# A decoder layer with sparse attention: one list schedule for the whole kernel, buffers that stay, and Strassen's algorithm in the second product of the MLP

## The chip, the cores and the metric

The kernel runs on one core of one Trainium2 chip. The metric is the time of one execution on the device in microseconds (us); the lower, the better. TensorE multiplies matrices into eight banks of PSUM, VectorE, ScalarE and GpSimd work on elements, and SyncE issues most DMAs.

## The reference

One decoder layer on 1024 tokens of width 1024, in float32. A conditioning vector gives shift, scale and gate for two sub-layers.

```
h    = rms_norm(x) * (1 + scale1) + shift1
proj = h @ w_in                              # queries, three kinds of keys and values, gates, convolution
attn = nsa_attention(...)                    # 8 heads: compressed, selected and windowed keys
conv = bgate * conv3(cgate * u)
x    = x + gate1 * (concat(attn, conv) @ w_out)
h2   = rms_norm(x) * (1 + scale2) + shift2
ff   = square(relu(h2 @ w_ff1)) @ w_ff2      # 1024 -> 4096 -> 1024
out  = x + gate2 * ff
```

## The kernel before

**Layout.** Everything is transposed: a tile has 128 channels on the partitions and tokens along the free dimension. The 1024 tokens are two halves of 512, called half 0 and half 1. A product in fp32 is made of three fast ones: each operand is split into a high part (a cast to fp32r, `P.copy`) and a low part (the operand less the high part, `P.sub`, on VectorE), and `mm3` issues high x high, high x low and low x high into one bank. So a tile of 128 x 512 with an inner dimension of 1024 is 8 x 3 = 24 matmuls of 128x128 by 128x512, and each tile of weights that comes by DMA costs a cast (ScalarE) and a subtraction (VectorE).

**Order of the work.** The code does not issue instructions itself. The calls `P.mm`, `P.act`, `P.tt`, `P.dma` and so on put operations into the plan (`class Plan`), with a cost for each engine on which they may run; the plan keeps which operation must follow which, from the regions of memory that they read and write, so that reusing a buffer makes an order too. `P.issue()` orders all the operations that have come since the last call: it runs a list schedule forward and one backward in turn, eight times, takes the time that was left to the end in one pass as the priority of the next, keeps the order with the shortest modelled span, and issues the instructions in it. Each engine then works through its own queue in order.

**Stages.** The plan is issued twice. The first plan holds the projections, the compressed keys and values, the convolution (`conv_fills`), the attention (`supers`: all of half 0, then half 1) and, as a filler that has no order of its own against the attention of half 1, `first_half`: for half 0 the output projection, the second norm, and tiles 2 to 31 of the hidden layer (`NFF = 30`), whose 128x512 results go to DRAM (`d_hid`). It ends with the output projection of half 1 (`out_proj`) and a copy of the eight tiles `x1h` (half 0 after the first sub-layer) into `FA1`. Then the pool `first` with the buffer `FA2` and the banks `sc`, `fa`, `po`, `stb` is closed, and new ones are opened: hidden tiles `hid` and the banks `pd`.

The second plan is the MLP. It finishes the second norm of half 1, and then goes through the hidden layer in four chunks of 8 tiles: `ff1` makes the tiles of half 1 (and tiles 0 and 1 of half 0; the others of half 0 come back from DRAM), each is split, and then eight output tiles are made for both halves with 24 matmuls each, and added with the gate `mod` into `x1` (`P.stt`, line 358 in the helper). In the first chunk `ada_cols` makes the last eight columns of the gates. After the fourth chunk the outputs are stored.

**Lines.** Nearly all operations are recorded in helpers: line 312 is a matmul, 315 a transposition, 336 a cast or copy on ScalarE, 338 on VectorE, 347 an addition, subtraction or product of two tensors on VectorE, 358 a product with a scalar and a sum on VectorE, 330 a function on ScalarE, 397 a DMA.

Of the kernel before, what the change touches and what calls it, by code (L numbers as in the profile page):

```python
# [10 lines left out]
F = mybir.dt.float32  # L11
R = mybir.dt.float32r
AF = mybir.ActivationFunctionType
ALU = mybir.AluOpType
PSUM = bass.MemoryType.PSUM
# [15 lines left out]
S_ = np.s_  # L31


def f32(ap):
    return ap.bitcast(F)
# [398 lines left out]
H0, H1, WR, RAN = 0, 8192, 16384, 16384 + 11328  # L434
AHEAD = {"silu": 30000}
FA1N, FA2N = 13316, 10752

NFF = 30


@with_exitstack
def hymba_layer(ctx: ExitStack, tc: tile.TileContext, xT, cT, w_first, w_cols, w_vg, w_ada, w_ada2, b_ada,
                norm1, norm2, qn, kn, pe, cw1, cw2, conv_w, rel_bias, onehot, ident_c, pair_c, w_out,
                w_ff1, w_ff2, out, dbg=None):
    nc = tc.nc
    P = Plan(tc)
    P.ahead = AHEAD
    mult, add, subt, amax, amin = ALU.mult, ALU.add, ALU.subtract, ALU.max, ALU.min
    EW = ("DVE",)

    def pool(stack, name, side="left", space=None):
        kw = {"space": space} if space else {"side": side}
        if space != DRAM:
            kw["reuse_waits"] = "tile"
        return stack.enter_context(tc.tile_pool(name=name, bufs=1, **kw))
# [7 lines left out]
    def mm3(ps, w, h, wsl, hsl, start, stop):  # L463
        P.mm(ps, w[0][wsl], h[0][hsl], start, False)
        P.mm(ps, w[0][wsl], h[1][hsl], False, False)
        P.mm(ps, w[1][wsl], h[0][hsl], False, stop)
# [9 lines left out]
    d_conv = [[dtile(f"d_conv{j}{i}", 128, 512) for i in range(2)] for j in range(4)]  # L476
# [3 lines left out]
    d_hid = [dtile(f"d_hid{j}", 128, 512) for j in range(32)]  # L480
# [8 lines left out]
    bones = ctile("bones", 128, dtype=R)  # L489
    mod, bad = ctile("mod", 48), ctile("bad", 48)  # L490
    n1, n2, a1, a2, c1, ct, sl = (ctile(n, 8) for n in ("n1", "n2", "a1", "a2", "c1", "ct", "sl"))
    qnr, qns, knr, kns, eps, one = (ctile(n, 1) for n in ("qnr", "qns", "knr", "kns", "eps", "one"))
    cvw = ctile("cvw", 4, 3)
    gates = ctile("gates", 8, 24)
    vc = [ctile(f"vc{g}", 128, dtype=R) for g in range(2)]
# [3 lines left out]
    RA = keep.tile([128, RAN], R, name="RA")  # L499
    FA1 = keep.tile([128, FA1N], F, name="FA1")  # L500
    first = ctx.enter_context(ExitStack())
    FA2 = pool(first, "first", side="right").tile([128, FA2N], F, name="FA2")
    psp = pool(first, "ps", space=PSUM)
    sc_t = [psp.tile([128, 512], F, name=f"sc{i}") for i in range(4)]
    fa_t = [psp.tile([128, 512], F, name=f"fa{i}") for i in range(2)]
    po_t, stb = psp.tile([128, 512], F, name="po"), psp.tile([128, 512], F, name="stb")
# [5 lines left out]
    h = [[Region(RA, H0 + 8192 * hf + 4096 * i, H0 + 8192 * hf + 4096 * i + 4096)(8, 512) for i in range(2)] for hf in range(2)]  # L512
# [7 lines left out]
    def rsqrt_neg2(y, t, ms):  # L520

        P.act(t, ms, AF.Ln, bias=eps[0:t.shape[0]])
        P.act(y, t, AF.Exp, scale=-0.5)
        P.act(t, y, AF.Square)
        P.stt(t, ms, EPS, t, add, mult)
        P.stt(y, t, -3.0, y, add, mult)
        return y
# [34 lines left out]
    def ada_cols(j0, n, stage, acc, bank):  # L562

        for k in range(8):
            wa = stage()[:, 0:128 * n]
            P.dma(wa, w_ada2[k, :, 128 * (j0 - 16):128 * (j0 - 16 + n)])
            if k == 0:
                P.act(acc, wa, AF.Copy, scale=sl[:, k:k + 1])
            elif k % 2 == 0:
                P.stt(acc, wa, sl[:, k:k + 1], acc, mult, add)  # L570
            else:
                P.act(wa, wa, AF.Copy, scale=sl[:, k:k + 1])
                P.tt(acc, acc, wa, add, EW)
        for i in range(n):
            P.mm(bank[:, i:i + 1], acc[:, 128 * i:128 * i + 128], one, True, True)
        P.tt(mod[:, j0:j0 + n], bank[:, 0:n], bad[:, j0:j0 + n], add)
# [42 lines left out]
    for k in range(8):  # L619
# [5 lines left out]
        ws = wfs_r()  # L625
# [32 lines left out]
    banks, cbanks = Rot(sc_t), Rot([po_t, fa_t[0], fa_t[1]])  # L658
# [195 lines left out]
    while c0 < TROW:  # L854
        n = min(512, TROW - c0)
        a = cbanks()
# [24 lines left out]
    Gr = Region(FA2, 0, FA2N - 640)  # L881
    x1h, at0 = [Gr(512) for _ in range(8)], [Gr(512) for _ in range(4)]
    ot_r, ada_acc, ada_r = Gr.rot(2, 256), Gr(512), Gr.rot(3, 512)
    cg_t, z_t, t1_t = ([Dr(n) for _ in range(2)] for n in (512, 514, 512))

    Wr = Region(RA, WR, RAN)
    fw0_r, hl_r, kall0, q0_r, vt0 = Wr.rot(3, 2, 512), Wr.rot(8, 512), Wr(KC0 + T), Wr.rot(2, 2, 2, 256), Wr(4, 2, 128)
    Wr = Region(RA, RAN - 4160, RAN)
# [180 lines left out]
    def norm2_apply(k, t, x, y, h2):  # L1069
        P.tt(t, x, y, mult, EW)  # L1070
        P.act(t, t, AF.Identity, bias=mod[:, 24 + k:25 + k], scale=a2[:, k:k + 1])
        P.copy(h2[0][:, k], t, ("DVE", "ACT"))
        P.sub(h2[1][:, k], t, f32(h2[0][:, k]), EW)

    def first_half():
# [33 lines left out]

        tiles = [(w_ff1[j], lambda a, j=j: put_hid(j, a)) for j in range(32 - NFF, 32)]  # L1110
        P.group = "ff"
# [44 lines left out]
                    pass  # L1156


    x1 = [[FA1[:, 1024 * c + 512 * hf:1024 * c + 512 * hf + 512] for hf in range(2)] for c in range(8)]
    h2 = [h[0], h[1]]  # L1160
    tmp, sacc = Rot(at0), t1_t[1]
    wt_r = Region(RA, RAN - 4160, RAN).rot(4, 2, 512)
    for c in range(8):
        P.dma(x1[c][1], xT[c, :, 512:1024])
# [6 lines left out]
    for k in range(4):  # L1171
        load_mix(1, k, [ada_acc, *ada_r.t][k], h[1][0][:, k], h[1][1][:, k])
    out_proj(wt_r, h[1], Rot(sc_t), done_second)
    for c in range(8):
        P.dma(x1[c][0], x1h[c])
    P.issue()
    if dbg:
        for i in range(2):
            nc.sync.dma_start(out=dbg["vc"][i], in_=f32(vc[i]))
        nc.sync.dma_start(out=dbg["gates"], in_=gates)  # L1180
        for p in range(4):
            for m in range(2):
                nc.sync.dma_start(out=dbg["conv"][p * 128:p * 128 + 128, m * 512:m * 512 + 512], in_=d_conv[p][m])
        for c in range(8):
            for hf in range(2):
                nc.sync.dma_start(out=dbg["x1"][:, c, hf * 512:hf * 512 + 512], in_=x1[c][hf])
    first.close()


    with ExitStack() as pf:  # L1190
        ff = pool(pf, "ff", side="right")
        psd = pool(pf, "psD", space=PSUM)
        banks = Rot([psd.tile([128, 512], F, name=f"pd{i}") for i in range(8)])
        Fr, Gr = Region(FA1, 8192, FA1N - 1536), Region(FA1, FA1N - 1024, FA1N)
        ws_r = Fr.rot(2, 8, 128)
        tmp, ff_acc = Rot([*Fr.rot(3, 512).t, Gr(512)]), Gr(512)
        w5 = [Region(RA, c, c + 1024)(8, 128) for c in (*range(RAN - 4160, RAN - 1023, 1024), WR)]
        wh_r, wl_r = Rot([w5[0], w5[2], w5[4]]), Rot([w5[1], w5[3]])
        Wr = Region(RA, WR + 1024, RAN - 4160)
        hids = [Wr(512) for _ in range(12)] + [ff.tile([128, 512], R, name=f"hid{i}") for i in range(20)]  # L1200
        hid = [[[hids[16 * hf + 2 * j + i] for hf in range(2)] for j in range(8)] for i in range(2)]

        def load_w(src):
            ws, hi, lo = ws_r(), wh_r(), wl_r()
            P.dma(ws, src)
            P.copy(hi, ws)
            P.sub(lo, ws, f32(hi), EW)
            return hi, lo

        def split_hid(j, hf, t):  # L1210
            P.copy(hid[0][j][hf], t, ("DVE",))
            P.sub(hid[1][j][hf], t, f32(hid[0][j][hf]), EW)

        def ff1(j, hf, w):
            a = banks()
            for k in range(8):
                mm3(a, w, h2[hf], S_[:, k], S_[:, k], k == 0, k == 7)
            t = tmp()
            P.act(t, a, AF.Relu)
            P.act(t, t, AF.Square)  # L1220
            split_hid(j, hf, t)

        st, y1 = banks(), ff_acc
        P.mm(st, f32(bones), sacc, True, True)
        rsqrt_neg2(y1, tmp(), st)
        for k in range(8):
            norm2_apply(k, tmp(), x1[k][1], y1, h[1])
        for ch in range(4):
            for j in range(8):
                w = load_w(w_ff1[ch * 8 + j])  # L1230
                if ch * 8 + j >= 32 - NFF:
                    t = tmp()
                    P.dma(t, d_hid[ch * 8 + j])
                    split_hid(j, 0, t)
                else:
                    ff1(j, 0, w)
                ff1(j, 1, w)
            if ch == 0:
                for i in range(2):
                    ada_cols(40 + 4 * i, 4, tmp, ff_acc, banks())  # L1240
            for c in range(8):
                w = load_w(w_ff2[ch, c])
                for hf in range(2):
                    a = banks()
                    for k in range(8):
                        hh = [hid[i][k][hf] for i in range(2)]
                        mm3(a, w, hh, S_[:, k], S_[:], k == 0, k == 7)
                    P.stt(x1[c][hf], a, mod[:, 40 + c:41 + c], x1[c][hf], mult, add)
                    if ch == 3:
                        P.dma(out[c, :, hf * 512:hf * 512 + 512], x1[c][hf])  # L1250
        P.issue()

# [78 lines left out]
```

## Time and profile before

| | before |
|---|---|
| time, median of 3 runs | 1353.28 us (1350.94 to 1354.62) |
| profiled execution | 1352.0 us, span 1350.2 us |
| TensorE busy | 1322.4 us (98%), 6424 matmuls |
| VectorE busy | 776.7 us (58%) |
| ScalarE busy | 626.6 us (46%) |
| mean granted clock of TensorE | 0.994 |
| DMA | 175.63 MB, mean 130 GB/s |

The span goes from the first to the last instruction of the profiled execution; the time contains what lies around it, too. A busy time is the union of an engine's instructions. Matmuls overlap in the records: one of 128x512 lasts some 0.39 us there, and the next starts before it ends, so the distance between starts says how dense TensorE is. The same holds, less strongly, on VectorE.

### The profile page before, as it was taken

Reading aid. Unit: us, or ns where it says so; the run is one execution under the profiler, and the core shown is the slowest. Engines: PE = TensorE matmul, PEld = TensorE weight load, DVE = VectorE, ACT = ScalarE, POOL = GpSimd, SP = SyncE. Lnnn points to the kernel's source line nnn. Section 1 sums busy time; section 2 is a strip of 40 time slices with the busy share of each in tenths; the row PEclk is TensorE's granted clock in tenths of the full one; section 3 lists DMA queues with packets and bytes.
Section 4 is the critical chain, followed back from the end, with each engine's and each line's share of the span. In section 5 each row is a group of like instructions: output and inputs, shape, how many; then the busy total and the mean of one; then the engine's idle time right before and its main releaser. Section 6 shows DMA issues by size and latency. Waiting matters only on the chain.

```text
span 1350.2 us, 18276 instructions
## 1 busy us (share of the span) xinstructions
PE 1322.4 (98%) x6424; PEld 1079.6 (80%) x6424; DVE 776.7 (58%) x1882; ACT 626.6 (46%) x1294; POOL 131.5 (10%) x239
## 2 busy tenths in 40 slices
PE   6999999999999999999999999999999999999998
PEld 2788788878878878888888877888888888888887
DVE  6998778868587696565655447543522342244312
ACT  6776677666565597565665435320221032103200
POOL 0001003222221112121112000000000000000000
PEclk9999999999999989999999999999999999999999
DMA  9488895444251315334225523532322241223231
GB/s 331 156 238 237 278 312 186 146 154 135 89 172 57 112 33 169 108 119 145 94 86 172 159 60 102 166 107 86 116 80 61 66 123 63 63 78 94 76 111 63
DMA packets 91601, 175.63 MB, mean 130 GB/s; under 512 B 10746, under 2 KB 30755, under 8 KB 90997
## 3 DMA queue, kind: packets, MB, share of 16 engines
q1 hardware_dynamic: 87764, 159.65, 37.7%
q0 software_dynamic: 3744, 14.81, 3.5%
q8 instruction: 50, 0.82, 0.2%
q14 instruction: 43, 0.34, 0.1%
HBM read 145.48 MB, written 32.61 MB: 132 GB/s over the span
## 4 chain that ended last, share of the span: by engine, by line
PE 88%; DVE 6%; DMA 3%; issue 1%; ACT 1%; SPq 0%; POOL 0%; DVEq 0%; ACTq 0%; POOLq 0%
PE pd L312 39%; PE fa L312 23%; PE sc L312 15%; PE po L312 6%; PE stb L315 3%; PE sc L315 2%; DVE FA L358 2%; DVE RA L347 1%; DVE FA L347 1%; ACT FA L330 1%; DVE FA L377 1%; DMA FA<-in_w_ada 1%; DMA d_tab<-d_row 0%; SPq L397 0%; DMA d_k<-FA 0%
## 5 line engine op out<-in xcount | busy, mean ns | idle before, releaser
L312 PE MATMUL fa<-RA 128*128 128x512 f32 (+1 forms) x1384 | 448.0, 410 | 1.0 <-DVE RA L338 0.7
L312 PE MATMUL pd<-RA 128*128 128x512 f32 x1392 | 409.0, 390 | 0.6 <-DVE RA L338 0.5
L336 ACT CAST RA<-FA 128x512 fp32r<-128x512 f32 (+5 forms) x237 | 163.8, 707 | 459.0 <-PE pd L312 273.0
L312 PE MATMUL sc<-RA 128*128 128x512 f32 (+7 forms) x1328 | 352.3, 367 | 6.8 <-ACT RA L336 2.6
L347 DVE TENSOR_TENSOR RA<-FA,RA 128x512 fp32r<-128x512 f32 (+5 forms) x327 | 248.9, 777 | 141.0 <-PE pd L312 68.4
L312 PE MATMUL pd<-hid,RA 128*128 128x512 f32 x960 | 309.7, 389 | 0.0
L312 PEld LDWEIGHTS pd<-RA 128*128 128x128 f32 x1392 | 261.0, 188 | 56.1 <-issue 1.4
L312 PEld LDWEIGHTS fa<-RA 128*128 128x128 f32 (+1 forms) x1384 | 249.0, 190 | 43.9 <-DVE RA L338 0.9
L312 PEld LDWEIGHTS sc<-RA 128*128 128x128 f32 x1328 | 234.7, 190 | 50.3 <-DVE RA L347 4.6
L312 PEld LDWEIGHTS pd<-hid,RA 128*128 128x128 f32 x960 | 180.2, 188 | 37.4
L358 DVE SCALAR_TENSOR_TENSOR FA<-pd,mod,FA 128x512 f32<-128x512 f32 x64 | 46.4, 746 | 199.8 <-PE pd L312 199.8
L312 PE MATMUL po<-RA 128*128 128x256 f32 (+2 forms) x564 | 140.2, 302 | 0.0
L330 ACT ACTIVATE FA<-FA,nm 128x64 f32<-128x64 f32 (+6 forms) x192 | 114.9, 601 | 24.4 <-DVE nm L366 23.7
L312 PEld LDWEIGHTS po<-RA 128*128 128x128 f32 (+1 forms) x564 | 102.4, 190 | 13.4 <-issue 0.2
L377 DVE CUSTOM_DVE_ANT_0 FA<-sc,FA 128x64 f32<-128x64 f32 (+5 forms) x192 | 84.6, 455 | 43.9 <-PE sc L312 41.3
L330 ACT ACTIVATE FA<-FA 128x512 f32<-128x512 f32 (+2 forms) x147 | 89.9, 619 | 22.3 <-DVE FA L358 12.4
L370 POOL TENSOR_SCALAR FA<-FA,cf 128x640 f32<-128x640 f32 (+8 forms) x115 | 72.6, 642 | 238.5 <-DVE cf L347 136.2
L315 PE MATMUL stb<-FA,FA 128*128 128x128 f32 (+1 forms) x304 | 76.7, 279 | 3.0 <-DVE RA L347 3.0
L347 DVE TENSOR_TENSOR RA<-stb,RA 128x512 fp32r<-128x512 f32 (+1 forms) x84 | 53.3, 635 | 27.9 <-PE po L312 13.2
L315 PE MATMUL sc<-FA,FA 128*128 128x128 f32 (+1 forms) x288 | 68.0, 276 | 0.0
L347 DVE TENSOR_TENSOR RA<-sc,RA 128x512 fp32r<-128x512 f32 (+2 forms) x84 | 51.1, 608 | 25.5 <-ACT RA L336 14.4
L336 ACT CAST RA<-sc 128x512 fp32r<-128x512 f32 (+2 forms) x84 | 43.6, 519 | 38.3 <-PE sc L315 35.3
(126 smaller groups left out, 909.8 us busy)
## 6 DMA issues: line engine op xcount, KB each, us to landing
FA<-in_w_ff SPq DMA_DIRECT2D x64, 512.0 KB, 3.7
FA<-in_w_ada SPq DMA_DIRECT2D x64, 256.0 KB, 3.2
FA<-in_w_ff SPq DMA_DIRECT2D x60, 256.0 KB, 3.0
FA<-in_w_cols SPq DMA_DIRECT2D x34, 256.0 KB, 3.2
FA<-in_xT SPq DMA_DIRECT2D x32, 256.0 KB, 5.2
FA<-in_w_ada SPq DMA_DIRECT2D x16, 512.0 KB, 6.8
d_q<-FA SPq DMA_DIRECT2D x32, 256.0 KB, 4.2
RA<-d_q POOLq DMA_DIRECT2D x16, 512.0 KB, 5.3
```

The lines of the kernel that those rows point to most:

```text
L312: self.op([("PE", c, lambda: self.nc.tensor.matmul(out, a, b, start=start, stop=stop))], [out], [a, b])
L315: self.op([("PE", 110.0, lambda: self.nc.tensor.transpose(out, a, ident))], [out], [a, ident])
L330: self.op([("ACT", c, lambda: self.nc.scalar.activation(out, a, func, **kw))], outs, ins)
L336: alts.append((e, 0.833 * n + (53 if ps else 93), lambda: self.nc.scalar.copy(out, a)))
L347: alts.append((e, 1.04 * n + 68, lambda: self.nc.vector.tensor_tensor(out, a, b, op)))
L358: self.op([("DVE", 1.04 * self._n(out) + 68 + 61 * ptr, lambda: self.nc.vector.scalar_tensor_tensor(out, a, s, b, op0, op1, **kw))], [out] ...
L370: alts.append((e, 0.833 * n + 174 + 83 * ptr, lambda: self.nc.gpsimd.tensor_scalar(out, a, s1, s2, op0, op1)))
L377: self.op([("DVE", 1.04 * self._n(out) + 75, lambda: self.nc.vector.tensor_tensor_reduce(out, a, b, 1.0, init, ALU.add, ALU.max, accum))], ...
```

## The change

There is one plan and one `P.issue()` for the whole kernel. The pool `first` is not closed; the MLP takes its buffers from regions of `RA`, `FA1` and `FA2`, and its banks are the eight of the first stage in rotation. The tiles `x1h` stay where they are. `NFF` is 32: all tiles of half 0's hidden layer are part of `first_half`, and the MLP's loop reads all of them from DRAM. The weights of the first product are loaded in two parts of 128x512 (4 inner tiles each) instead of one of 128x1024.

The second product of a chunk is made by Strassen's algorithm (in the form with seven products and combinations that are used again). The chunk's weights are a 2 x 2 matrix of quarters (inner tiles 0 to 3 and 4 to 7, output tiles 0 to 3 and 4 to 7), the hidden tiles too (`b11`, `b21` are half 0, `b12`, `b22` half 1, inner tiles 0 to 3 and 4 to 7). In each of seven rounds four right-hand tiles are split (`split_b`), for each of four output tiles a quarter of weights is loaded and, in four rounds, added to or subtracted from another, split, and multiplied (`product`: 4 inner tiles, 12 matmuls). The bank is added with the gate into one or two output tiles, or into `u2`, which gathers the sum of the first and fourth rounds over all chunks and is added to three quarters of the output in the last chunk.

```diff
-NFF = 30
+NFF = 32
...
-    x1 = [[FA1[:, 1024 * c + 512 * hf:1024 * c + 512 * hf + 512] for hf in range(2)] for c in range(8)]
+    x1 = [[x1h[c], FA1[:, 512 * c:512 * c + 512]] for c in range(8)]
...
-    tmp, sacc = Rot(at0), t1_t[1]
+    tmp, sacc = Region(FA1, 4096, 6144).rot(4, 512), t1_t[1]
...
-    for c in range(8):
-        P.dma(x1[c][0], x1h[c])
-    P.issue()
-    first.close()
...
+    banks = Rot([*sc_t, *fa_t, po_t, stb])
+    raw = [at0 + Region(FA2, 6144, 8192).rot(4, 512).t, Region(FA1, 4096, 8192).rot(8, 512).t]
+    Fr = Region(FA2, 8192, FA2N)
+    u2, y1 = Fr.rot(4, 512).t, Fr(512)
+    Fr = Region(FA1, 8192, 12288)
+    st_r, S = Fr.rot(4, 512), Fr.rot(4, 512).t
+    st_r = Rot(st_r.t + Region(FA1, FA1N - 1024, FA1N).rot(2, 512).t)
+    Wr = Region(RA, WR, RAN)
+    w_r = Wr.rot(14, 512)
+    b_r = Rot([Wr(2, 4, 512), *Region(RA, H0, H0 + 8192).rot(2, 2, 4, 512).t])
+    def split(t):
+        hi, lo = w_r(), w_r()
+        P.copy(hi, t)
+        P.sub(lo, t, f32(hi), EW)
+        return [x.rearrange("p (k n) -> p k n", k=4) for x in (hi, lo)]
...
+    def split_b(tiles):
+        b = b_r()
+        for k, t in enumerate(tiles):
+            P.copy(b[:, 0, k], t, ("ACT", "DVE"))
+            P.sub(b[:, 1, k], t, f32(b[:, 0, k]), EW)
+        return b[:, 0], b[:, 1]
+    def product(w, x):
+        a = banks()
+        for k in range(4):
+            mm3(a, w, x, S_[:, k], S_[:, k], k == 0, k == 3)
+        return a
+    def ff1(j, hfs):
+        a = {hf: banks() for hf in hfs}
+        for kk in range(2):
+            w = split(load(st_r(), w_ff1[j][:, 4 * kk:4 * kk + 4]))
+            for hf in hfs:
+                for k in range(4):
+                    mm3(a[hf], w, h2[hf], S_[:, k], S_[:, 4 * kk + k], kk + k == 0, kk == 1 and k == 3)
+        for hf in hfs:
+            t = raw[hf][j % 8]
+            P.act(t, a[hf], AF.Relu)
+            P.act(t, t, AF.Square)
+    def to_out(c, hf, bank, sign=mod):
+        g = ng[:, c - 4:c - 3] if sign is ng else mod[:, 40 + c:41 + c]
+        P.stt(x1[c][hf], bank, g, x1[c][hf], mult, add)
...
+    for ch in range(4):
+        for j in range(8 * ch, 8 * ch + 8):
+            if j >= 32 - NFF:
+                P.dma(raw[0][j % 8], d_hid[j])
+                ff1(j, (1,))
...
+        if ch == 0:
+            for i in range(2):
+                ada_cols(40 + 4 * i, 4, st_r, y1, banks())
+            P.ts(ng, mod[:, 44:48], -1.0, None, mult)
+        b11, b12, b21, b22 = raw[0][0:4], raw[1][0:4], raw[0][4:8], raw[1][4:8]
+        def quad(c, f, k, t=None):
+            return load(st_r() if t is None else t, w_ff2[ch, c + 4 * f][:, 4 * k:4 * k + 4])
+        x = split_b(b11)
+        for c in range(4):
+            a = product(split(quad(c, 0, 0)), x)
+            if ch == 0:
+                P.copy(u2[c], a, ("DVE",))
+            else:
+                P.tt(u2[c], a, u2[c], add)
+            to_out(c, 0, a)
+        x = split_b(b21)
+        for c in range(4):
+            to_out(c, 0, product(split(quad(c, 0, 1)), x))
+            if ch == 3:
+                store(c, 0)
+        for k in range(4):
+            P.tt(b11[k], b12[k], b11[k], subt)
+        x = split_b(b11)
+        for c in range(4):
+            P.tt(S[c], quad(c, 1, 0, S[c]), quad(c, 1, 1), add)
+            a = product(split(S[c]), x)
+            to_out(c + 4, 1, a)
+            to_out(c, 1, a)
+        for k in range(4):
+            P.tt(b11[k], b22[k], b11[k], subt)
+        x = split_b(b11)
+        for c in range(4):
+            P.tt(S[c], S[c], quad(c, 0, 0), subt)
+            P.tt(u2[c], product(split(S[c]), x), u2[c], add)
+            if ch == 3:
+                to_out(c, 1, u2[c])
+                for hf in range(2):
+                    to_out(c + 4, hf, u2[c])
+        x = split_b(b22)
+        for c in range(4):
+            P.tt(S[c], quad(c, 0, 1), S[c], subt)
+            to_out(c, 1, product(split(S[c]), x))
...
+        for k in range(4):
+            P.tt(b12[k], b22[k], b12[k], subt)
+        x = split_b(b12)
+        for c in range(4):
+            t = quad(c, 0, 0)
+            P.tt(t, t, quad(c, 1, 0), subt)
+            a = product(split(t), x)
+            for hf in range(2):
+                to_out(c + 4, hf, a)
...
+        for k in range(4):
+            P.tt(b21[k], b11[k], b21[k], subt)
+        x = split_b(b21)
+        for c in range(4):
+            to_out(c + 4, 0, product(split(quad(c, 1, 1)), x), ng)
...
+    P.issue()
```

## Rows read from the trace of the kernel before

**Rows 1.** Stretches: span, busy TensorE, weight loads, VectorE, ScalarE, GpSimd, clock, DMA, GB/s.

```profile
33.80:67.50 33.70, 31.57 (x130) 23.62 (x129) 32.21 (x68) 25.18 (x45) 0.53 (x4) 0.97 0.50 156
67.50:101.20 33.70, 33.53 (x188) 28.58 (x187) 30.70 (x71) 23.96 (x52) 2.39 (x4) 1.00 0.84 238
...
202.00:472.00 270.00, 269.31 (x1464) 219.87 (x1463) 201.49 (x657) 166.93 (x436) 66.25 (x124) 1.00 0.41 132
472.00:510.00 38.00, 35.03 (x192) 28.68 (x191) 36.85 (x111) 34.17 (x72) 4.98 (x8) 0.91 0.15 47
510.00:805.80 295.80, 295.80 (x1557) 244.55 (x1555) 165.40 (x440) 167.88 (x349) 46.45 (x72) 1.00 0.38 122
...
816.00:1346.00 530.00, 529.92 (x2346) 438.49 (x2344) 201.53 (x287) 115.23 (x150) 0.00 (x0) 1.00 0.30 90
```

**Rows 2.** Groups of instructions, 816 to 1346 us: count, busy us, mean ns, idle before.

```profile
L312 PE MATMUL pd<-RA 128*128 128x512 f32 x1370 | 403.1, 389 | 0.5 <-DVE RA L338 0.5
L312 PE MATMUL pd<-hid,RA 128*128 128x512 f32 x960 | 309.7, 389 | 0.0
...
L358 DVE SCALAR_TENSOR_TENSOR FA<-pd,mod,FA 128x512 f32<-128x512 f32 x64 | 46.4, 746 | 199.8 <-PE pd L312 199.8
L347 DVE TENSOR_TENSOR hid<-FA,hid 128x512 fp32r<-128x512 f32 x40 | 27.1, 690 | 0.9
...
L330 ACT ACTIVATE FA<-pd 128x512 f32<-128x512 f32 x34 | 19.5, 586 | 1.4 <-PE pd L312 1.4
L338 DVE CAST hid<-FA 128x512 fp32r<-128x512 f32 x40 | 16.4, 422 | 3.0 <-DMA FA<-d_hid 3.0
...
L336 ACT CAST RA<-FA 128x512 fp32r<-128x512 f32 x4 | 2.5, 614 | 0.1
```

**Rows 3.** Timeline of TensorE near the end, start and us; 23 matmuls between.

```profile
1334.65 0.39 PE L312 MATMUL pd<-hid,RA 128*128 128x512 f32 x1
...
1340.09 5.83 PE L312 MATMUL pd<-hid,RA 128*128 128x512 f32 x25
```

**Rows 4.** Chain of waits at the seam: start, us, what.

```profile
804.49 0.75 DVE FA L358
...
815.58 530.35 PE pd L312 x2346
```

**Rows 5.** Timeline of TensorE, its gaps: idle time and releaser in brackets.

```profile
486.17 0.79 PE L315 MATMUL stb<-FA,FA 128*128 128x128 f32 x4 [2.95 <-DVE RA L347]
...
808.57 1.10 PE L312 MATMUL pd<-FA,bones 128*128 128x512 f32 x2 [2.76 <-DVE FA L347]
...
815.58 14.80 PE L312 MATMUL pd<-RA 128*128 128x512 f32 x64 [0.52 <-DVE RA L338]
```

**Rows 6.** Timeline of VectorE where it is never idle.

```profile
500.58 0.42 DVE L338 CAST RA<-FA 128x512 fp32r<-128x512 f32 x1
500.91 0.69 DVE L347 TENSOR_TENSOR FA<-FA,FA 128x512 f32<-128x512 f32 x1
...
503.20 1.89 DVE L347 TENSOR_TENSOR RA<-FA,RA 128x512 fp32r<-128x512 f32 x3
505.01 0.61 DVE L377 CUSTOM_DVE_ANT_0 FA<-sc,FA 128x448 f32<-128x448 f32 x1
...
891.18 0.74 DVE L358 SCALAR_TENSOR_TENSOR FA<-FA,sl 128x512 f32<-128x512 f32 x1
891.84 0.75 DVE L358 SCALAR_TENSOR_TENSOR FA<-pd,mod,FA 128x512 f32<-128x512 f32 x1
892.50 0.69 DVE L347 TENSOR_TENSOR FA<-FA 128x512 f32<-128x512 f32 x1
```

**Rows 7.** Timeline of VectorE at the second norm, its first cast and last subtraction.

```profile
815.02 0.42 DVE L338 CAST RA<-FA 128x512 fp32r<-128x512 f32 x1
...
826.12 0.69 DVE L347 TENSOR_TENSOR RA<-FA,RA 128x512 fp32r<-128x512 f32 x1
```

**Rows 8.** DMA issues: count, KB each, median us from issue to landing.

```profile
FA<-in_w_ff SPq DMA_DIRECT2D x64, 512.0 KB, 3.7
...
FA<-in_w_ff SPq DMA_DIRECT2D x60, 256.0 KB, 3.0
...
FA<-d_hid SPq DMA_DIRECT2D x30, 256.0 KB, 2.6
```

More of the change, by code (lines that the diff above doesn't have):

```diff
@@ L1173, in hymba_layer @@
     out_proj(wt_r, h[1], Rot(sc_t), done_second)
-    for c in range(8):
-        P.dma(x1[c][0], x1h[c])
-    P.issue()
[L1177 to L1186, printed above, removed]
@@ L1187, in hymba_layer @@
-    first.close()
[L1190 to L1250, printed above, removed]
-        P.issue()
@@ new lines, in hymba_layer @@
+    P.group = "mlp"
+    banks = Rot([*sc_t, *fa_t, po_t, stb])
[8 more added lines that the diff above has]
+    b_r = Rot([Wr(2, 4, 512), *Region(RA, H0, H0 + 8192).rot(2, 2, 4, 512).t])
@@ new lines, in split, with load @@
+    def split(t):
[3 more added lines that the diff above has]
+        return [x.rearrange("p (k n) -> p k n", k=4) for x in (hi, lo)]
+    def load(t, src):
+        P.dma(t.rearrange("p (k n) -> p k n", k=4), src)
+        return t
+    def split_b(tiles):
[4 more added lines that the diff above has]
+        return b[:, 0], b[:, 1]
@@ new lines, in to_out, with store @@
+    def to_out(c, hf, bank, sign=mod):
+        g = ng[:, c - 4:c - 3] if sign is ng else mod[:, 40 + c:41 + c]
+        P.stt(x1[c][hf], bank, g, x1[c][hf], mult, add)
+    def store(c, hf):
+        P.dma(out[c, :, hf * 512:hf * 512 + 512], x1[c][hf])
+    ng = a1[:, 0:4]
+    st = banks()
+    P.mm(st, f32(bones), sacc, True, True)
+    rsqrt_neg2(y1, st_r(), st)
+    for k in range(8):
+        norm2_apply(k, st_r(), x1[k][1], y1, h[1])
+    for ch in range(4):
[4 more added lines that the diff above has]
+            else:
+                ff1(j, (0,))
+                ff1(j, (1,))
+        if ch == 0:
[10 more added lines that the diff above has]
+                P.copy(u2[c], a, ("DVE",))
+            else:
+                P.tt(u2[c], a, u2[c], add)
[27 more added lines that the diff above has]
+            to_out(c, 1, product(split(S[c]), x))
+            if ch == 3:
+                store(c, 1)
+        for k in range(4):
[7 more added lines that the diff above has]
+                to_out(c + 4, hf, a)
+            if ch == 3:
+                store(c + 4, 1)
+        for k in range(4):
[3 more added lines that the diff above has]
+            to_out(c + 4, 0, product(split(quad(c, 1, 1)), x), ng)
+            if ch == 3:
+                store(c + 4, 0)
```

## The prediction

> **What bounds the kernel now.** I read the table of stretches first. In it the reader is to see which engine is full in each stage: TensorE is busy for 529.92 of the 530.0 us from 816 on (the MLP of half 1), for all of 510 to 805.8, and for 269.31 of 270 us before that, at clock 1.00; VectorE is busy for 38% of the MLP, for 56% of 510 to 805.8 and for 75% of 202 to 472 [rows 1]. A busy TensorE need not be a dense one, so I next take the spacing of its matmuls: from 1334.65 to 1340.09 us 24 products of 128x512 start, 5.44 us / 24 = 0.2267 us each [rows 3]. The groups of the MLP count 1370 + 960 of them, and 2330 x 0.2267 = 528.2 of 530 us [rows 2]: that stretch is dense, and nothing but fewer columns makes it shorter. The chain of waits says the same: it stays on one line of TensorE for 530.35 us [rows 4]. In the whole timeline of TensorE I then look for gaps near what the change touches. There are two at the seam of the two schedules, 2.76 us before the matmul of the second norm's statistics and 0.52 us before the MLP goes dense, and one of 2.95 us at 486 us [rows 5], in a stretch where VectorE is busy 36.85 of 38 us and the granted clock is 0.91 [rows 1].
>
> **The change part by part.**
>
> *Fewer matmuls.* Before, the second product of a chunk (a quarter of the hidden layer, 8 tiles of 128) is 8 output tiles x 2 halves x 8 inner tiles x 3 = 384 matmuls. After, it is 7 rounds x 4 output tiles x 4 inner tiles x 3 = 336. So 4 x 48 = 192 fall away, all in the dense stretch: 192 x 0.2267 = **43.5 us**. The spacing stays: the new products have the same 128x512 form, and runs of 12 and 24 per bank differ only in how often the bank changes.
>
> *The two inner tiles of half 0.* Their 48 matmuls move from behind the seam to the stage before it. 48 x 0.2267 = 10.9 us on a full TensorE on either side: 0.
>
> *The seam.* One schedule takes the end of the first pool, the eight copies of x1h and the barrier out. What remains is a chain of data: the last output tile, its square and sum, the statistics matmul, the norm, the first cast of h2; from the add at 804.49 to the first product at 815.58 [rows 4]. Two tiles of half 0 fill 10.9 us of it. Before, they could not start until the second schedule did, and 2.76 + 0.52 = 3.3 us stayed empty. From the buffers, the last three of the now 32 tiles (29, 30, 31) may still run beside this chain: tile 28 is the last to use the buffer in which the norm's sum gathers. Three tiles are 16.3 us, more than the chain. Later than before is the pace of h2 itself: its first cast starts at 815.02 and its last tile is done at 826.81 [rows 7], eight in some 11 us, 1.4 us each against 0.68 us for the three matmuls that use one; but four inner tiles can have weights ready, 4 x 0.68 = 2.7 us per step, so it hides. Bounds: all 3.3 us back, or, if the planner spends all tiles earlier, the whole 805.8 to 815.58 less the 1.1 us of the statistics is empty, 8.7 us instead of 3.3, 5.4 worse. I take the 3.3 back, since a plan made for the whole kernel pays for this gap and the old one didn't.
>
> *VectorE in the MLP.* This is what the change costs. Spacing in a dense stretch: three 128x512 subtractions and the next start in 1.81 us, **0.605** each; an add with a scalar from a bank 0.66; a cast 0.33 [rows 6]. Per chunk, in the seven rounds: 28 subtractions for weights, 28 for the right-hand sides, 16 sums of these, 16 of weights, 8 on u2: 96 x 0.605 = 58.1; 32 scaled adds x 0.665 = 21.3. Sum 79.4 us beside 336 x 0.2267 = 76.2 us of TensorE. If all 28 casts of right-hand sides fall to VectorE, 9.2 more; ScalarE has room for them (72 casts and 16 pairs for the inner tiles, 104 x 0.6 = 62 us of 119.7 [rows 2]). The first product of a chunk costs 192 x 0.2267 = 43.5 us of TensorE and 16 x 0.605 = 9.7 us of VectorE. So a chunk is 89 to 98 us of VectorE in 119.7 us: 74 to 82%. The rounds alone are over 100%, so the rest must run ahead or behind: seven pairs of weight buffers (7 x 0.605) and three of right-hand sides (12 + 4 operations) let 23 x 0.605 = 13.9 us run ahead during the first product, and eight banks let evictions trail. Then 65.5 to 75 of 76.2 us are left, and every round has its slack. The last chunk has 12 more adds (8.0 us) and no first product behind it: 73.5 to 83. What VectorE at such shares does to TensorE: at 75%, 0.69 us lost in 270; at 91%, 0.17 in 33.7; at 96% (33.8 to 67.5), 2.1 in 33.7; and at 97% the 2.95 of 38 us with the clock down [rows 1]. Bounds: 0 (TensorE is at its spacing already, so no gain) to the excess in the rivals. I take the 91% row, as a chunk lies under it: 0.17 / 33.7 of 478 us = **2.4 us**.
>
> [...] This trace has the 0.69 us as duration, but starts 0.605 us apart [rows 2, 6], so by the trace the sum keeps 0.605.
>
> *Transfers.* Weights of the second product come in 36 loads of 256 KB per chunk, not 8 of 512 KB. With 16 for the first product and 8 of hidden tiles that is 60 in 119.7 us, 15.7 MB, 131 GB/s; the MLP moves 90 now, and 202 to 472 us moved 132 with TensorE full [rows 1]. A load lands in 3.0 us, a hidden tile in 2.6 [rows 8], and six buffers of 2.7 us each lie ahead: 0. In chunk 0 the 16 loads for the last gates pass the same six buffers; their sums (some 16 steps of 0.7 us) lie beside the 43.5 us of the first product: 0, at most the 3 us of one load.
>
> *A new order of the first stage.* Every priority is worked out anew. No MLP work can enter before 800 us but the two tiles, so the work is the same; the order may fill the valley at 472 to 510 us or dig another. Bounds from its row: idle 2.97 plus 38 x 0.09 of clock = 6.4 us, either way. I take 0.
>
> Sum against the profiled execution (1352.0 us, span 1350.2): 1352.0 - 43.5 - 3.3 + 2.4 = 1307.6. It is 1.3 us under the median of the runs shown, so **1309 us** is the forecast.
>
> **The rivals.**
>
> A: The seam stays or grows. For it: in the old plan a tile of half 0 ran beside the last output tiles although a gap followed; against it: the old plan ended there. From +3.3 to +8.7 against the forecast: 1312 to 1318.
>
> B: VectorE trails in part. If the run-ahead reaches half (7 us) and half the casts land on it: 79.4 + 4.6 - 7 - 76.2 = 0.8 us a chunk, and 8 more in the last: 11 us, less the 2.4 already taken: 1318. For it: rounds 3 and 6 want 8 scaled adds each, and 16 more operations behind these.
>
> C: Every VectorE operation holds the engine for its whole duration (0.69 and 0.746 [rows 2]): 96 x 0.69 + 32 x 0.746 = 90.1; half the casts at 0.42, 5.9; less 23 x 0.69 = 15.9: 80.1, so 3.9 late in three chunks and 12.9 in the last, 24.6 us: 1331. Against it: the spacing measured. [...]
>
> D, slower: VectorE becomes the bound of the rounds. If nothing runs ahead (the sums of right-hand sides wait for the round before them, in buffers they overwrite) and all casts land on VectorE, a chunk's rounds take 79.4 + 9.2 = 88.6 us instead of 76.2, 12.4 x 4 + 8 = 58 us: 1352.0 - 46.8 + 58 + 1.3 = 1364. It decides against the change from (43.5 + 3.3) / 4 = 11.7 us a chunk. Against it: three sets of right-hand sides and seven of weights, and ScalarE's free half.
>
> E: The new order fills the valley: down to 1302, with less stall 1300.
>
> **How the numbers follow.** Forecast 0.64 (1303 to 1313), A 0.09, B 0.10, C 0.05, D 0.04, E 0.08. Up to 2 in 10 left out: the range is 1299 to 1327, from E to beyond B, cutting off C and D. A measurement of this kernel can tell 0.3%, 4 us. Slower by that is D alone, 0.04; within it 0.02, the upper end of C; faster 0.94.
>
> **What would show it.** 1344 products of rounds and 6232 matmuls in all (6424 - 192); TensorE's spacing 0.2267 from the seam to the end, some 478 us; no idle before the statistics matmul; VectorE at 75 to 85% in the MLP with little of TensorE's idle time released by it. Wrong would be: gaps of TensorE released by VectorE in every chunk, worst in the last; the statistics matmul with an empty 9 us around it; or a first stage that ends later than 806 + 11 us.

## The result and the profile after

The changed kernel takes 1317.16 us (median of 4 runs, 1315.25 to 1318.86) against 1353.83 us before (4 runs, 1350.94 to 1354.62): ratio 0.9732, 95% interval 0.9713 to 0.9752. The forecast was 1309, with a range to 1327. So 36.7 us came of the 44 foretold.

The page of the changed kernel, busy time of each engine (share of the span of 1313.5 us) and number of instructions, and the granted clock in 40 slices:

```profile
PE 1281.3 (98%) x6232; PEld 1043.1 (79%) x6232; DVE 975.2 (74%) x2230; ACT 731.4 (56%) x1518; POOL 124.1 (9%) x232
...
PEclk8999999999999999999999999899999999999999
```

There are 192 matmuls fewer, as the diff says. VectorE works 198.5 us more than before, and one slice of the clock in the middle, the 26th, is low. The stretches, with the columns of [rows 1]:

```profile
202.00:472.00 270.00, 268.86 (x1447) 218.94 (x1447) 204.20 (x646) 175.38 (x452) 56.03 (x111) 1.00 0.41 132
472.00:510.00 38.00, 37.16 (x210) 30.19 (x209) 35.76 (x106) 32.61 (x69) 7.95 (x11) 1.00 0.21 66
510.00:805.80 295.80, 295.80 (x1565) 244.50 (x1564) 169.97 (x454) 170.74 (x354) 46.53 (x74) 1.00 0.38 121
...
815.20:826.20 11.00, 0.03 (x2) 0.00 (x1) 10.32 (x18) 9.98 (x18) 0.00 (x0) 0.61 0.51 168
...
838.20:1305.00 466.80, 466.80 (x2068) 386.85 (x2068) 370.97 (x595) 198.18 (x333) 0.00 (x0) 1.00 0.43 135
...
826.20:832.00 5.80, 5.80 (x15) 4.26 (x16) 5.48 (x10) 4.86 (x8) 0.00 (x0) 0.57 0.81 262
```

The reader is to see three things. From 838.2 to 1305 us TensorE is busy for all of 466.80 us with VectorE at 79% beside it. The valley at 472 to 510 us is mostly gone (37.16 instead of 35.03, clock 1.00 instead of 0.91). And from 815.2 to 826.2 us, at the seam, TensorE does nothing, and is granted 0.57 of its clock in the 5.8 us behind it. The timeline of TensorE there, which answers to [rows 5], and SyncE's issues in the same stretch:

```profile
769.76 39.38 PE L312 MATMUL sc<-RA 128*128 128x512 f32 x173
808.97 4.25 PE L312 MATMUL fa<-RA 128*128 128x512 f32 x18
813.06 1.02 PE L312 MATMUL sc<-FA,bones 128*128 128x512 f32 x2
813.51 1.71 PE L312 MATMUL fa<-RA 128*128 128x512 f32 x5
826.20 12.00 PE L312 MATMUL sc<-RA 128*128 128x512 f32 x41 [10.97 <-ACT RA L336]
...
814.11 0.33 SPq L397 DMA_DIRECT2D FA<-in_w_ff  x1
817.50 0.84 SPq L397 DMA_DIRECT2D d_hid<-FA  x2
821.46 18.28 SPq L397 DMA_DIRECT2D FA<-in_w_ff  x18
```

The output projection of half 1 (`sc<-RA`) runs alone and dense, 173 matmuls in a row. One tile of half 0 (`fa<-RA`, 18 and 5 records of its 24) is left behind it. It fills the wait for the statistics, so the gap of 2.76 us that stood there before is gone, but it ends at 815.2 us, and nothing is left for the rest of the second norm's chain. The weights of the MLP, one load apart, are asked for from 821.46 us on; before, they were from 807.10 us on. The chain of waits, which answers to [rows 4], ends at a cast of ScalarE (pieces between are left out):

```profile
813.22 0.87 PE sc L312 x2
...
814.12 0.69 ACT FA L330
...
817.95 1.90 DVE FA L347 x3
819.85 0.34 DVE RA L338
...
825.01 1.15 ACT RA L336 x2
...
826.20 3.92 PE sc L312 x8
```

The groups of the MLP, 838 to 1305 us, with the columns of [rows 2]:

```profile
L347 DVE TENSOR_TENSOR RA<-FA,RA 128x512 fp32r<-128x512 f32 x272 | 178.9, 684 | 72.0 <-ACT RA L336 31.1 <-issue 23.1 <-PE sc L312 10.6
L336 ACT CAST RA<-FA 128x512 fp32r<-128x512 f32 x259 | 155.3, 621 | 226.6 <-PE sc L312 97.2 <-PE po L312 44.0 <-PE fa L312 40.8
...
L347 DVE TENSOR_TENSOR FA<-FA 128x512 f32<-128x512 f32 x96 | 63.2, 682 | 0.4 <-DMA FA<-in_w_ff 0.3
```

Nearly all casts went to ScalarE, and VectorE itself waits for ScalarE and for TensorE: it is not the bound.

### The profile page after: what moved, and what is told of

Its sections match the earlier page's. It is cut to its first block, busy times and chain, and to the rows that moved or that the text cites. A ratio compares the mean times of both kernels' runs of the same rounds, so it can differ in the third digit from the quotient of the medians.

```text
span 1313.5 us, 18989 instructions
## 1 busy us (share of the span) xinstructions
PE 1281.3 (98%) x6232; PEld 1043.1 (79%) x6232; DVE 975.2 (74%) x2230; ACT 731.4 (56%) x1518; POOL 124.1 (9%) x232
## 4 chain that ended last, share of the span: by engine, by line
PE 88%; DVE 6%; DMA 3%; ACT 1%; SPq 1%; issue 1%; DVEq 0%; ACTq 0%
PE sc L312 34%; PE fa L312 34%; PE po L312 11%; PE stb L312 5%; PE stb L315 3%; PE sc L315 2%; DVE RA L347 2%; DVE FA L358 1%; DVE FA L347 1%; DMA FA<-in_xT 1%; SPq L397 1%; DMA d_q<-FA 1%; ACT FA L330 1%; DVE FA L377 1%; DMA FA<-in_cw 1%
## 5 line engine op out<-in xcount | busy, mean ns | idle before, releaser
L312 PE MATMUL sc<-RA 128*128 128x512 f32 (+4 forms) x2384 | 655.9, 378 | 16.7 <-ACT RA L336 13.8
L312 PE MATMUL fa<-RA 128*128 128x512 f32 (+1 forms) x1960 | 639.8, 404 | 1.3 <-DVE RA L347 0.6
L312 PEld LDWEIGHTS sc<-RA 128*128 128x128 f32 x2384 | 433.1, 189 | 103.8 <-ACT RA L336 15.6
L347 DVE TENSOR_TENSOR RA<-FA,RA 128x512 fp32r<-128x512 f32 (+3 forms) x531 | 348.2, 678 | 132.1 <-ACT RA L336 53.9
L336 ACT CAST RA<-FA 128x512 fp32r<-128x512 f32 (+3 forms) x450 | 262.5, 605 | 317.8 <-PE sc L312 127.4
L312 PEld LDWEIGHTS fa<-RA 128*128 128x128 f32 (+1 forms) x1960 | 356.4, 189 | 67.4 <-DVE RA L347 2.2
L312 PE MATMUL po<-RA 128*128 128x256 f32 (+3 forms) x828 | 241.1, 330 | 0.0
L330 ACT ACTIVATE FA<-FA,nm 128x64 f32<-128x64 f32 (+4 forms) x192 | 114.8, 600 | 29.9 <-DVE nm L366 29.6
L312 PE MATMUL stb<-RA 128*128 128x512 f32 x280 | 108.6, 391 | 0.5 <-DVE FA L358 0.4
L347 DVE TENSOR_TENSOR FA<-FA 128x512 f32<-128x512 f32 (+2 forms) x148 | 96.7, 671 | 4.4 <-ACT FA L330 3.0
```

Source lines behind the costliest of these rows:

```text
L312: self.op([("PE", c, lambda: self.nc.tensor.matmul(out, a, b, start=start, stop=stop))], [out], [a, b])
L330: self.op([("ACT", c, lambda: self.nc.scalar.activation(out, a, func, **kw))], outs, ins)
L336: alts.append((e, 0.833 * n + (53 if ps else 93), lambda: self.nc.scalar.copy(out, a)))
L347: alts.append((e, 1.04 * n + 68, lambda: self.nc.vector.tensor_tensor(out, a, b, op)))
```

## The experiments

Three questions were open: why the seam is empty, whether Strassen's rounds give all that they leave out, and how near VectorE is to binding. All times are medians; each kernel was timed beside the kernel before, whose medians were 1353.65 (e1 to e4), 1355.31 (e5 to e8) and 1354.35 us (e9, e10). Beside the changed kernel it was 1353.83, so 1.5 us of what e5 to e8 are slower than the changed kernel is not theirs. An edit anywhere also makes a new plan for the first stage: the statistics' matmul starts at 813.06 us in the changed kernel, at 815.75 in e1, 815.95 in e5, 815.74 in e6 and 814.95 in e8. Differences of 3 us between two kernels are therefore read from the stretch in question, not from the time.

### e1: the norm's scratch apart from the weights' buffers

The six buffers `st_r` take the weights, but also the scratch of the second norm: one use for the statistics, eight for the tiles of h2, and only then the first load.

```diff
-    rsqrt_neg2(y1, st_r(), st)
+    nt_r = Rot(raw[1][4:8])
+    rsqrt_neg2(y1, nt_r(), st)
     for k in range(8):
-        norm2_apply(k, st_r(), x1[k][1], y1, h[1])
+        norm2_apply(k, nt_r(), x1[k][1], y1, h[1])
```

> The second norm's scratch leaves the six buffers of the MLP's weights and goes to four tiles that are free then; nothing else. Two theories of the empty 10.97 us at the seam. Buffers: the first product waits for its weights, whose load waits for scratch in the same rotation. The first tile of h2 is whole at 821.4 in the changed kernel, and a product can follow some 0.9 us later, at 822.3 instead of 826.2: the gap shrinks by 3.9 us to 7, the time from 1317 to about 1313. Tiles: h2's own chain and the lack of other work make the whole gap: it stays at 11 us, the time within 2 us of 1317. A third, that VectorE's load at the norm holds h2 back, says the same as the second.

1312.13 us (1311.18 to 1314.3), ratio 0.9698 (0.968 to 0.9716). TensorE's timeline, then the stretch behind the gap:

```profile
815.75 1.02 PE L312 MATMUL sc<-FA,bones 128*128 128x512 f32 x2
816.21 1.71 PE L312 MATMUL fa<-RA 128*128 128x512 f32 x5
823.42 12.37 PE L312 MATMUL sc<-RA 128*128 128x512 f32 x41 [5.50 <-DVE RA L338]
...
820.00:832.00 12.00, 8.58 (x26) 6.81 (x26) 11.90 (x22) 10.58 (x17) 0.00 (x0) 0.72 0.39 146
```

The gap halves, 10.97 to 5.50 us, and what ends it is no longer ScalarE's cast but VectorE's cast of h2 (line 338 of the helper). Seven loads of weights are issued from 803.35 to 819.46 us, where the changed kernel issues one. So half of the gap was weights that waited behind the norm's scratch, as the first theory has it. The rest is the norm's chain with nothing beside it. The clock behind the gap is as low as before: 0.50 in the 5.8 us from 823.42 us on, against 0.57 in the same length behind the whole gap.

### e2 and e3: two tiles of half 0 behind the seam, without and with e1's edit

```diff
-NFF = 32
+NFF = 30
```

> NFF = 30: tiles 0 and 1 of half 0 are made inside the MLP again, all else as in the changed kernel. Tiles: 48 matmuls (10.9 us) that need no h2 of half 1 stand behind the seam, the gap of 10.97 us closes but for the statistics, the clock stays up: 1317 - 11 - 2.5 = 1303 to 1307. Buffers: the weights of these two tiles go through the same six buffers behind the norm's scratch, so they come no earlier than before: the gap stays above 8 us and the time within 4 us of 1317.

> Both edits: scratch apart and NFF = 30. Buffers and tiles together: weights are there when the output projection ends, two tiles fill the chain; the gap falls below 2 us and the slow clock behind it goes: 1317 - 10 - 2.5 = about 1304.5. If tiles alone were the cause, the same as with NFF = 30 alone. If buffers alone, the same as with the scratch apart alone, 1313. If VectorE's load at the norm sets the pace, no better than 1313 either.

e2: 1327.25 us (1325.24 to 1328.03), ratio 0.9805 (0.9787 to 0.9823). e3: 1305.84 us (1304.0 to 1307.98), ratio 0.965 (0.9631 to 0.9669). TensorE at the seam in e2, with the start of its span:

```profile
814.07 1.71 PE L312 MATMUL fa<-RA 128*128 128x512 f32 x5
826.92 12.98 PE L312 MATMUL sc<-RA 128*128 128x512 f32 x47 [11.14 <-ACT RA L336]
...
0.00:202.00 202.00, 180.34 (x803) 138.88 (x804) 159.99 (x369) 131.66 (x269) 11.08 (x33) 0.94 0.81 246
...
472.00:510.00 38.00, 34.68 (x191) 28.53 (x190) 34.58 (x107) 29.04 (x62) 5.04 (x8) 0.91 0.11 35
```

and in e3:

```profile
807.77 1.02 PE L312 MATMUL sc<-FA,bones 128*128 128x512 f32 x2
...
809.32 9.00 PE L312 MATMUL sc<-RA 128*128 128x512 f32 x39
...
822.02 4.15 PE L312 MATMUL sc<-RA 128*128 128x512 f32 x17 [0.52 <-DVE RA L347]
...
780.00:840.00 60.00, 59.48 (x260) 48.33 (x259) 40.63 (x68) 33.54 (x59) 0.00 (x0) 1.00 0.31 97
```

In e2 48 matmuls that need nothing of half 1 stand behind the seam and the gap is 11.14 us all the same: their weights come through the same six buffers, and 16 loads of them are issued from 822.04 us on. With those buffers free (e3) six loads are issued from 788.75 to 811.10 us, the same 48 matmuls run while the norm is made, 0.52 us stay empty, and the clock stays at 1.00. Neither edit closes the gap alone; both theories were right for a half. That e2 is 10 us slower than the changed kernel was not expected. The statistics' matmul starts at 813.62 us there, although the 10.9 us of two tiles are no longer ahead of it: the first stage lost some 11 us, in the first 202 us (180.34 us of TensorE instead of 186.69) and in the old valley, which is back. Why this order of the first stage is worse wasn't tried. The valley at 472 to 510 us does not go with the single plan: it is there with `NFF = 30` (before, e2, and 35.03 us of TensorE in e3) and filled in every kernel with 32, the two plans of e7 too (37.14 us).

### e4 and e10: three and five tiles, with e1's edit

`NFF = 29` and `NFF = 27`.

> Scratch apart and NFF = 29: three tiles behind the seam, 16.3 us of matmuls. If two tiles already cover the chain, 0 to 2 us from e3; if h2's pace (1.4 us per tile) still leaves holes behind two tiles, 2 to 5 us faster than e3: 1299 to 1302.

> Scratch apart and NFF = 27: five tiles of half 0 in the MLP instead of the three of e4. The seam is covered by three, the matmuls are the same in number: within 2.5 us of e4's 1303. If what e4 gained over e3 was more work behind the seam (and not the order of the first stage), again 2 to 3 us faster.

e4: 1302.98 us (1300.37 to 1305.14), ratio 0.9632 (0.9606 to 0.9657). e10: 1300.19 us (1299.4 to 1301.08), ratio 0.96 (0.9585 to 0.9614): the fastest of all. The seam of e4, then of e10 with its valley:

```profile
780.00:840.00 60.00, 60.00 (x265) 49.34 (x264) 42.78 (x70) 37.39 (x64) 1.01 (x1) 1.00 0.33 106
```

```profile
472.00:510.00 38.00, 37.34 (x211) 30.08 (x210) 35.37 (x104) 31.93 (x68) 9.58 (x12) 1.00 0.22 62
780.00:840.00 60.00, 60.00 (x265) 49.34 (x264) 40.28 (x69) 38.53 (x65) 0.00 (x0) 1.00 0.37 116
```

With three tiles TensorE is busy for all of 780 to 840 us, so more tiles can give nothing there. e4 is 2.9 us faster than e3, a difference that was foretold for holes behind two tiles; but e3's holes are 0.52 us, so that reason does not carry it. The valley has a clock of 1.00 in e4 and 0.91 in e3, and the intervals of the two ratios overlap. e10's 2.8 us over e4 are a little more than was expected without a cause at the seam; they would have to lie in the first stage, but the two profiled executions differ by 0.3 us (spans 1299.3 and 1299.0), and e4's runs by 4.8. This stays open.

### e9: the last three tiles of half 0 last in priority

On top of e1, `NFF` stays 32.

```diff
-AHEAD = {"silu": 30000}
+AHEAD = {"silu": 30000, "late": -100000}
...
-        yield from products([tiles[0:2], *([t] for t in tiles[2:])], rot, h0)
+        yield from products([tiles[0:2], *([t] for t in tiles[2:29])], rot, h0)
+        P.group = "late"
+        yield from products([[t] for t in tiles[29:]], rot, h0)
```

> On top of the scratch apart (e1): the last three tiles of half 0 get a lower priority than all else in the plan; NFF stays 32. If priorities spent the tiles before the seam, these three now stay for it, the remaining gap of 5.5 us and its slow clock go: about 1305. If the plan is greedy and a tile runs whenever TensorE has nothing else ready, however low its priority, they run beside the attention and the output projection all the same: gap 5 to 6 us, time within 2 us of e1 (1312).

1312.12 us (1309.54 to 1312.87), ratio 0.9683 (0.967 to 0.97), the time of e1. TensorE:

```profile
757.75 8.82 PE L312 MATMUL fa<-RA 128*128 128x512 f32 x38
...
810.37 4.25 PE L312 MATMUL fa<-RA 128*128 128x512 f32 x18
...
822.43 12.37 PE L312 MATMUL sc<-RA 128*128 128x512 f32 x41 [6.03 <-DVE RA L338]
```

From 757.75 us on, where the attention ends and the output projection has not begun, 38 matmuls of two of these tiles run in a row, though they come last in priority. The third runs behind the output projection, as one tile did in the changed kernel and in e1. This list schedule does not save work for a gap that is still ahead: it fills the one at hand. Why the third tile came late was not tried. The tiles of e3 come behind the norm in program order, and take their weights' buffers and banks there; by the code, that is what binds them.

### e5: the plain second product in the same buffers

```diff
...
+        for (k, hf), bb in (((0, 0), b11), ((1, 0), b21), ((0, 1), b12), ((1, 1), b22)):
+            x = split_b(bb)
+            for c in range(8):
+                to_out(c, hf, product(split(quad(c % 4, c // 4, k)), x))
+                if ch == 3 and k == 1:
+                    store(c, hf)
```

in place of the seven rounds.

> The changed kernel with the plain second product in the same buffers and the same single plan: per chunk 32 products of 12 matmuls (8 output tiles x 2 halves x 2 quarters of the inner dimension) instead of 28. If Strassen's seven rounds give all that they leave out, 192 x 0.2267 = 43.5 us more: 1360.7, slower than before. If VectorE's extra work in the rounds had cost TensorE something, less than that: 1350 to 1357. The gap at the seam stays at 11 us in both.

1361.93 us (2 runs, 1361.63 to 1362.23), ratio 1.0053 (1.0033 to 1.0073), 44.8 us over the changed kernel, or 43.3 without the 1.5. The gap at the seam and a stretch of the MLP, with VectorE at half its time and TensorE just as full:

```profile
829.09 11.89 PE L312 MATMUL sc<-RA 128*128 128x512 f32 x41 [10.98 <-ACT RA L336]
...
840.00:1305.00 465.00, 465.00 (x2061) 385.25 (x2060) 235.84 (x377) 156.91 (x271) 0.00 (x0) 1.00 0.37 114
```

From the first product behind the gap to TensorE's last, e5 takes 526.7 us (829.09 to 1355.83) and the changed kernel 483.4 (826.20 to 1309.55), 43.4 more. So the rounds give the whole 43.5 us of their 192 matmuls. Without them the rest of the change (one plan, kept buffers, `NFF = 32`, halved loads) is some 7 us slower than the kernel before. That is no verdict on the single plan: the seam alone is 10.2 us longer than before, and with the rounds two plans are slower than one (e7).

### e6: all casts of the MLP on VectorE

```diff
-            P.copy(b[:, 0, k], t, ("ACT", "DVE"))
+            P.copy(b[:, 0, k], t, ("DVE",))
...
-        P.copy(hi, t)
+        P.copy(hi, t, ("DVE",))
```

> All casts of the MLP's weights and right-hand sides go to VectorE: some 270 more at 0.33 us, 90 us on top of 371 in 467, so about 99% busy. If a mean under 100% is enough because buffers run ahead, the loss is small: 1317 to 1322, all of it in the last chunk. If the rounds bind on their own (over 100% of a round for 5 of 7), TensorE starves in every chunk: 1330 to 1350.

1324.95 us (1324.37 to 1325.95), ratio 0.9781 (0.9766 to 0.9795). The MLP, then the last instructions of TensorE and VectorE:

```profile
840.00:1305.00 465.00, 465.00 (x2061) 385.24 (x2060) 442.74 (x838) 45.56 (x74) 0.00 (x0) 1.00 0.43 136
...
1310.86 2.43 PE L312 MATMUL sc<-RA 128*128 128x512 f32 x10
...
1318.39 2.06 DVE L358 SCALAR_TENSOR_TENSOR FA<-sc,a,FA 128x512 f32<-128x512 f32 x3
```

With VectorE at 95% TensorE is still never idle in the MLP. VectorE ends 7.2 us after TensorE (0.8 in the changed kernel), and these 6.4 us are what the medians lose (7.8 us, 6.3 without the 1.5). The profiled execution loses 3.7 us more ahead of 840 us: the statistics start 2.7 us later, and the gap behind them, now ended by a cast of VectorE, is 11.90 us. The first theory holds for the rounds; the time is 3 us over its figure.

### e7: two plans

```diff
+    P.issue()
     P.group = "mlp"
```

> The plan is issued twice again, with a cut before the second norm of half 1; buffers, tiles and rounds as in the changed kernel. If the single plan is worth the old seam (3.3 us) and the early loads of weights, hidden tiles and their splits: 3 to 8 us slower, 1320 to 1325, with a longer gap at the seam. If the single plan gains nothing, because the gap is one of buffers: within 2 us of 1317.

1323.6 us (1322.03 to 1324.78), ratio 0.9769 (0.9755 to 0.9784), 6.4 us slower than the changed kernel, 5.0 without the 1.5. TensorE:

```profile
819.30 1.13 PE L312 MATMUL sc<-FA,bones 128*128 128x512 f32 x2 [2.24 <-DVE FA L347]
833.55 11.79 PE L312 MATMUL sc<-RA 128*128 128x512 f32 x39 [13.12 <-ACT RA L336]
```

The cut makes both gaps, 2.24 and 13.12 us, where the single plan has one of 10.97. So the single plan gives back what the prediction says of it, and somewhat more: 4.4 us of idle time, with one tile of half 0 running up to and behind the statistics. The long gap is not its doing.

### e8: three pairs of weight buffers instead of seven

```diff
-    w_r = Wr.rot(14, 512)
+    w_r = Rot(Wr.rot(14, 512).t[:6])
```

> Three pairs of weight buffers instead of seven. If the run-ahead is what hides VectorE in the rounds, TensorE gets gaps in the rounds of every chunk (weights wait for the product three before, 8.2 us, and a load, a cast, a subtraction and for four rounds a sum take some 6 us of it) and where the last gates' loads pass the same six buffers in chunk 0: 1325 to 1340. If each product's own 2.7 us is enough, 1317 to 1320.

1329.5 us (1328.4 to 1330.01), ratio 0.9815 (0.9798 to 0.9831). The time is as expected, the place is not. TensorE's timeline and two stretches:

```profile
883.56 1.01 PE L312 MATMUL sc<-one,FA 128*128 128x1 f32 x4 [7.66 <-DVE FA L347]
...
880.00:890.00 10.00, 6.44 (x20) 5.31 (x21) 5.12 (x8) 2.55 (x4) 0.00 (x0) 0.57 0.78 240
...
960.00:1080.00 120.00, 120.00 (x531) 99.38 (x530) 93.09 (x150) 49.50 (x83) 0.00 (x0) 1.00 0.41 133
```

From 840 to 1305 us there is one gap, in the first chunk, where the loads of the last gates pass the six buffers of the weights' loads: TensorE waits for their sums 7.66 us, and goes on at a clock of 0.57 (5.8 us from 883.56 us on). The gates' loads are issued from 857.04 us on, in the changed kernel one at 842.87 and the others from 847.32 on. The rounds themselves run without a gap on three pairs. What seven pairs buy is the cover for the gates' chain, not the rounds.

## Why the prediction was right and where it failed

The forecast was 8 us too low and the time lies in its range, but that is in part luck: one term was off by 13.5 us, and three smaller ones went the other way.

**Fewer matmuls: right.** 43.5 us foretold; e5 shows some 43 when they are put back. The spacing stayed: TensorE is busy through 466.80 us in the MLP, and from 838 to 1305 us its 2053 records of 128x512, at 0.2267 us each, make 465.4 of the 467 us.

**The seam: wrong, and it is the term that failed.** The prediction took back the 3.3 us of [rows 5], "since a plan made for the whole kernel pays for this gap". Measured is a gap of 10.97 us, and behind it 42 matmuls in 12.0 us where 42 x 0.2267 = 9.5, so 2.5 us of clock: 13.5 us instead of 3.3 before, +10.2 in place of -3.3. One of its signs did come true: there is no idle time before the statistics. From their matmul to the first product of h2, though, it is 13.1 us (813.06 to 826.20) where it was 7.0 (808.57 to 815.58); in e1, with the scratch apart, it is 7.7. Two links failed. That three tiles "may still run beside this chain" is only leave: two of the three were spent before the output projection, even when they come last in priority (e9), and the one that stayed ended at 815.2 us. And the prediction did not look at who else uses the six weight buffers: it priced the norm's chain and counted on weights being there (e1, e2). Rival A was this case, with 0.09 far too unlikely, and too small: it had the empty chain (8.7 us), not the buffers behind it nor the clock. The trace of the kernel before could have warned of this: of the two tiles of half 0 that the prediction has filling 10.9 us there, only one lies in the gap,

```profile
809.10 5.96 PE L312 MATMUL pd<-RA 128*128 128x512 f32 x22
```

and the first product of half 1 follows it at 815.58 us.

**VectorE: right in its load, too careful in its price.** 74 to 82% foretold, 79% measured; 2.4 us of stall foretold, none measured. e6 shows the margin: at 95% only the end of the last chunk suffers. The explanation by seven weight pairs was wrong in part (e8: three do for the rounds). The spacing decides: in e6 the durations of VectorE's 838 operations from 840 to 1305 us add up to 508 us, more than the 465 us in which it did them, so they overlap, and rival C, which assumes that each holds the engine for its whole duration, is not what happens here. The starts 0.605 us apart of operations of 0.69 us agree with that [rows 6], and so does e6 itself: four subtractions of 0.68 us each, from 1284.61 us on, and the next start is at 1287.02 us, 2.41 us / 4 = 0.60. B and D fall because TensorE never waits in the MLP. ScalarE was counted too high: a chunk has 8 pairs for the inner tiles, not 16, so 88 x 0.6 = 53 us and not 62; 198.18 of 466.80 us are 51 of 119.7.

**The two tiles and the first stage.** Taken at 0. The first stage, less the two tiles and the statistics, ends at 815.2 - 10.9 - 1.0 = 803.3 us instead of 805.8, 2.5 us better, with the valley nearly filled: rival E in part. It is no more than what a new plan moves this stage by in e1, e5 and e6.

**Transfers: 0, right.** The loads carried 135 GB/s with TensorE full.

Sum of what failed: +13.5 at the seam, -2.4 of stall not needed, -2.5 in the first stage, -0.9 in the end of the span and rounding: 7.7 us, the profiled execution's 1315.25 against 1307.6.

## What to carry to other kernels

This list schedule filled the gap that it had, not the one to come; whoever counts on fill work for a later gap must bind it there, by its place in the program order or its buffers, and check that everything this work needs (its weights' buffers as well) is free by then. Before a rotation of buffers is shared, list all its users in program order around the stage's start: nine uses of scratch ahead of the first load cost as much here as the missing fill. And an algorithm that trades matmuls for elementwise work paid in full here, with the elementwise engine's load, counted by the spacing of its instructions, under the matmuls' time per chunk (79% of it); the last chunk, which has nothing behind it, needs a look of its own.

## What the hardware showed that was not expected

A VectorE at 95% of 465 us beside a TensorE that is never idle. And the price of a gap lies partly behind it. In the 5.8 us that follow a gap of TensorE the granted clock was 0.57 after 10.97 us of idle time (changed kernel), 0.57 after 7.66 (e8), 0.50 after 6.03 (e9) and 0.50 after 5.50 (e1): half the gap did not halve this price. In the changed kernel the 0.57 is a mean: the clock was 0.50 from 826.2 to 831.0 us, 0.89 from 831.0 to 832.0 us, and 1.00 from there on. After the 0.52 us of e3 it stayed at 1.00. In the kernel before it stayed at 1.00 after 2.76 us, where TensorE had been busy for all of 510 to 805.8 us, and was 0.53 after 2.95 us at 486 us, where it had been busy for 11.20 of 14.17 us. So the length of a gap alone did not tell its price here.
